# One gate projection of a hybrid decoder layer moved from the opening into the last three query pairs of the attention

## The chip, the cores and the metric

The kernel runs on one core of a Trainium2 chip. A core has a matrix engine (PE, TensorE), a vector engine (DVE), a scalar engine (ACT, ScalarE), a general engine (POOL, GpSimd) and an engine that here only issues transfers (SP, SyncE). Each engine takes its instructions in a fixed order and waits at the head of its queue for what an instruction needs. The metric is the device time of one execution in microseconds (us); lower is better.

## The reference, cut to what matters

One layer runs on a prompt of 1,024 tokens and on 8 sequences of 4 new tokens (1,056 tokens in all). A combined input projection feeds an attention and a gated recurrence; a shared output projection and a feed-forward part follow. The change touches `lg`, the gate of the recurrence:

```
u = rmsnorm(x, p['g_norm1']) * (1 + sc1) + sh1
proj = u @ p['w_in']
q, k, v, lx, lg = jnp.split(proj, [...], axis=-1)
...
hs, h_last = rg_lru(xc, h0, p['w_rgate'], ..., p['lru_lambda'])
lru_out = (hs * jax.nn.gelu(lg.astype(F32), approximate=True)).astype(dt)
m = jnp.concatenate([attn_out, lru_out], axis=-1) @ p['w_out']
```

`lg` has 512 channels, so four tiles of 128 channels; each is a projection of its own, and only `lru_out`, the second half of the input of the output projection, needs it. The recurrence `hs` itself does not.

## The kernel before, in words

Every float32 operand of a projection is kept as a high and a low half, and every product is made of three matmuls (lines 156 to 158). `Weights` takes the weight matrices ("units") one after another in a fixed list: it loads a unit raw, splits it on ScalarE (`w_hi`, line 60) and GpSimd (`w_lo`), and puts the halves into one of four slots, chosen by the unit's place in the list. A projection of one gate tile covers 128 channels and all 1,056 tokens, in three token chunks of 384, 384 and 288 (`TC`): 8 products of 3 matmuls for each chunk, 72 matmuls in all.

The program runs in this order, and a scheduler that weighs times beforehand fixes each engine's order:

1. The opening: normalisation, input projections of the recurrence (`lx`), gate projections (`pj`), the two value blocks (`v_ps`), the first query and key groups (`qk_ps`). The recurrence runs behind it tile by tile: gate matmuls `pg`, chains of elementwise work, a scan (line 541). `proj(4)`, `proj(7)` and `proj(10)` project gate tiles 0, 1 and 2 there, `gelu(n, b)` takes the gelu on ScalarE (line 551), and `lru_out(n)` multiplies it by the scanned `T2[n]` on DVE (lines 557 to 561) and stores the product in `scr_l[n]`. Tile 3's scan is stored alone, in `scr_h` (line 590).
2. The attention over 16 query pairs g = 0 to 15 (4 heads of 4 pairs; a later pair of a head sees more keys). `score` makes the scores `s_ps` (lines 804 to 806), ScalarE takes the exponential `p_e` (line 813), DVE combines the two halves, PE transposes them (`qk_pt`, line 834), and `pv` multiplies them by the values (`pv_ps`). Two banks hold scores, so the next scores wait until an exponential has read its bank. Up to pair 12 the gaps of a pair are filled with matmuls of the queries and keys of pair g + 3 (`qk_mm`). The last pairs have no such fill. Gate tile 3 fills there instead: `lg_piece` projects half of the inner dimension of one token chunk into a bank named `qk_ps`, and after the second half takes the gelu (tile `gl`, line 869) and stores it in `scr_l[3]`. Chunk 0 is put into pair 14 and chunks 1 and 2 into pair 15.
3. The output projection (`wo_k`, `wo_ps`). `lru_cat_stage` brings the recurrence's half of its input back for a token chunk: for each tile m it loads `cat` from `scr_l[m]`, for m = 3 also `hs` from `scr_h`, multiplies the two on DVE (line 998) and splits the product into `act_h` (ScalarE, line 1000) and `act_l` (line 1001). Chunk 0 is staged during the last pairs, chunks 1 and 2 later, with a two-buffer pool that `cat` and `hs` share. The key pages of the 32 new tokens (`kp`, line 1004) are loaded in the same stretch on SP's queue, into buffers that hold parts of the projection's input until the last gate piece has read them.
4. The feed-forward part, over half of the span.

Exponential and gelu use different tables of ScalarE: each change between them is an `ACT_TABLE_LOAD` in the trace.

Of the kernel before, what the change touches and what calls it, by code (L numbers as in the profile page):

```python
# [6 lines left out]
F32 = mybir.dt.float32  # L7
# [9 lines left out]
SEQ = 1024  # L17
NS = 8
DT = 4
# [20 lines left out]
class Weights:  # L40
# [12 lines left out]
    def split_to(self, n, eng=None):  # L53
        while len(self.parts) < min(n, len(self.units)):
            i = len(self.parts)
            self.dma_to(i + 1)
            s = i % 4 if i < 12 else 2 if i == 12 else (3, 2, 0, 1)[(i - 13) % 4]
            hi = self.pool.tile([128, 1024], F32R, name="w_hi", tag=f"w_hi{s}", bufs=1)
            lo = self.pool.tile([128, 1024], F32R, name="w_lo", tag=f"w_lo{s}", bufs=1)
            self.nc.scalar.activation(hi, self.raw[i], AF.Copy)  # L60
            (eng or self.nc.gpsimd).tensor_tensor(lo, self.raw[i], hi.bitcast(F32), op=ALU.subtract)  # L61
            self.parts.append((hi, lo))
            self.dma_to(i + 1 + RAW)
# [82 lines left out]
class Build:  # L146
# [25 lines left out]

    def run(self):
        a = self.a
        units = [a["w_in"][i] for i in (0, 1, 2, 3, 4, 7, 8, 5, 11, 12, 6, 9, 10, *range(13, 20))] + [a["w_out"][i] for i in (4, 5, 6, 7, 0, 1, 2, 3)]
        order = [("u", 0), ("u", 1), ("u", 2), ("u", 3)]
        for b in range(NFF // 2):
            if b + 1 < NFF // 2:
                order += [("u", 4 * b + 4), ("u", 4 * b + 5)]
            order += [("d", 2 * b), ("d", 2 * b + 1)]  # L180
            if b + 1 < NFF // 2:
                order += [("u", 4 * b + 6), ("u", 4 * b + 7)]
        self.ffn_unit = {o: len(units) + i for i, o in enumerate(order)}
        units += [a["w_up"][i] if t == "u" else a["w_down"][i] for t, i in order]
        with self.pool("const") as cp, self.pool("weights") as wp, self.pool("acts") as ap_:
            self.cp, self.ap, self.act = cp, ap_, {}
            self.W = Weights(self.nc, wp, units)
            self.front()
            self.output()
# [13 lines left out]
    def front(self):  # L203
# [362 lines left out]
        def lru():  # L566
            yield from conv(0)
            yield from conv_split(0)
            yield from conv(1)
            yield from gates(0)  # L570
            yield from conv_split(1)
            yield from chain(0)
            while 2 not in X:
                yield None
            yield from conv(2)
            yield from gates(1)
            yield from conv_split(2)
            yield from chain(1)
            yield from gates(2)
            yield from lru_out(0)  # L580
            while 3 not in X:
                yield None
            yield from conv(3)
            yield from conv_split(3)
            yield from lru_out(1)
            yield from chain(2)
            yield from gates(3)
            yield from lru_out(2)
            yield from chain(3)
            SP.dma_start(a["scr_h"], T2[3])  # L590

        W.split_to(4)
        evac(0, lx01[0])
# [50 lines left out]
            return b.rearrange("p (x c) -> p x c", x=2)  # L644

        def v_block(bl, hook):
            unit = (5, 11)[bl]
            vh, vl = (v01[bl][:, z] for z in range(2))
            for pr in range(4):
                p = two(bank("v_ps", "mm", MM[0]))  # L650
                for x in range(2):
                    for hf in range(2):
                        project_half(p, x, 2 * pr + x, unit, hf)
                st = stage("v_st")
                S.activation(st, p, AF.Copy)
                S.dma_start(a["v_o"][pr][:, :, bl * 256:(bl + 1) * 256], st)
                S.activation(vh[:, 2 * pr:2 * pr + 2], p, AF.Copy)
                V.tensor_tensor(vl[:, 2 * pr:2 * pr + 2], p, vh[:, 2 * pr:2 * pr + 2].bitcast(F32),
                                op=ALU.subtract)
                hook(pr)  # L660
            p = two(bank("v_ps", "mm", MM[0]))
            for hf in range(2):
                project_half(p, 0, 8, unit, hf)
            S.activation(self.vsn[:, bl * 256:(bl + 1) * 256], p[:SAMP, 0], AF.Copy)

        v_block(0, lambda pr: None)
        W.split_to(11)
        b = proj(7)
        gelu(1, b)
        W.split_to(12)  # L670
        gqk = self.load(vp, "g_qk", [128, 2, 64])
        cs = self.load(vp, "rope", [128, 9, 2, 16])
        g64 = "p x (g d) -> p (x g) d"
# [36 lines left out]
        tbank = [lambda: bank("qk_pt", "mm", MM[0])]  # L710

        def qk_unit(h):
            return 11 + 2 * h if h else 8

        def qk_mm(g, piece):

# [34 lines left out]
        for g in range(3):  # L751
            for i in range(4):
                qk_mm(g, i)
            qk_norm(g)
            if g == 1:
                b = proj(10)
                bg.until(lambda: 3 in T2 and len(done) >= 6)
                gelu(2, b)
                W.split_to(13)
        bg.finish()  # L760
        lpp.__exit__(None, None, None)
        SP.dma_start(a["lru_h_o"], lho)
# [15 lines left out]
        SP.dma_start(mk, a["maskT"])  # L778
        G.tensor_copy(idb, ident)
        G.tensor_copy(mkb, mk)  # L780
        W.split_to(15)
        qk_T(0)
        psp.__exit__(None, None, None)

# [71 lines left out]
                S.activation(ot, PO.pop(g), AF.Copy)  # L856
                S.dma_start(a["scr_o"][h][:, pr * 256:(pr + 1) * 256], ot)

        def lg_piece(i, half):
            t0, tw = TC[i]  # L860
            hi, lo = W.get(19, NK)
            if half == 0:
                PS["lg"] = qbank[0]()
            b = PS["lg"]
# [2 lines left out]
            if half:  # L867
                t = stage("gl3").rearrange("p x c -> p (x c)")
                S.activation(t[:, :tw], b[:, :tw], AF.Gelu_apprx_tanh)
                S.dma_start(a["scr_l"][3][:, t0:t0 + tw], t[:, :tw])  # L870

        NG = 4 * H
        for _ in range(2):
# [3 lines left out]
        for g in range(NG):  # L877
            h, pr = divmod(g, 4)
            if g + 3 < NG:
                fill = [lambda i=i: qk_mm(g + 3, i) for i in range(4)]  # L880
            else:
                fill = [lambda i=i, j=j: lg_piece(j, i) for j in ((),(0,),(1,2))[g + 3 - NG] for i in range(2)]
            nT = (g - 1) % 4 + 1 if g else 0
            Ts = [lambda b=b: pv_T(g - 1, b) for b in range(nT)]
            Ps = [lambda b=b: pv(g - 1, b) for b in range(nT)]
# [5 lines left out]
            if pr == 2:  # L891
                b = qbank[0]()
                for hf in range(2):
                    project_half(two(b[:, :512]), 0, 8, qk_unit(h), hf)
                W.split_to((17, 19, 21, 23)[h])
                ss = stage("qk_ss")
                ys = sums(b[:SAMP, None, :256], 1, SAMP, ss[:SAMP, 0:1])
            if h < 2:
# [6 lines left out]
            if g == 9:  # L905
                self.x2 = [x2p.tile([128, 4, T], F32, name="x2a", tag="v", bufs=1)]
                SP.dma_start(self.x2[0], a["xT"][0:4].rearrange("m p t -> p m t"))
            if g == NG - 1:
                early = [self.lru_cat_load(0, stage, m) for m in range(2)]
            score(g, 0, 0)  # L910
            score(g, 0, 1)
# [72 lines left out]
    def lru_cat_stage(self, i, stage, early=()):  # L984
# [3 lines left out]
        s = slice(t0, t0 + tw)  # L988
        for m in range(4):
            t = early[m] if m < len(early) else self.lru_cat_load(i, stage, m)  # L990
            if m == 3:
                hs = stage("hs3").rearrange("p x c -> p (x c)")[:, :tw]
                SP.dma_start(hs[:, :w], a["scr_h"][:, t0:t0 + w])
                if tw > w:
                    sv = bass.AP(tensor=a["scr_h"].tensor, offset=a["scr_h"].offset + SEQ + 3,
                                 ap=[[LO, 128], [7, NS], [1, DT]])
                    SP.dma_start(hs[:, w:].rearrange("p (s q) -> p s q", s=NS), sv)
                V.tensor_tensor(t, t, hs, op=ALU.mult)
            hi, lo = self.act_at(4 + m, s)
# [663 lines left out]
```

## Time and profile before

| what | before |
|---|---|
| runs of the kernel | 1361.44, 1362.48 and 1366.3 us, median 1362.48 |
| the profiled execution: its own time | 1362.76 us |
| the profiled execution: its span in the trace | 1360.2 us |
| granted clock of PE, mean | 0.995 |
| PE, DVE, ACT, POOL busy | 1312.9, 777.0, 552.1, 480.0 us |
| last exponential of pair 15 ends | 439.10 us |
| output projection's second group begins | 453.86 us |

The span runs from the first to the last instruction that the profiler recorded; the profiled execution's own time is 2.56 us longer. Times within the trace, such as 439.10, are counted from the span's start. Busy shares are means over stages that differ a lot, so the rows below are read stage by stage.

### The profile page before, as it was taken

The page shows a single profiled execution, that of the slowest core. Times are in us where ns is not written, and L with a number is a line of the kernel's source. Part 1 is how long each engine was busy: PE and PEld are TensorE (multiplying, and loading weights), DVE is VectorE, ACT ScalarE, POOL GpSimd, SP SyncE. Part 2 cuts the span into 40 slices and gives each one's busy share as a digit, 9 for nine tenths or more (in the row PEclk, how much of TensorE's full clock was granted, in tenths as well). Part 3 has the DMA queues.
Part 4 walks back from the last instruction along what each step waited for, and adds up shares of the span by engine and source line. Part 5 has one row for each costly group of instructions (what it writes and reads, how often), then busy time and mean ns, then how long its engine had stood idle before and what let it go on. Part 6 is the DMA issues. An engine that isn't in the chain of part 4 may idle for free.

```text
span 1360.2 us, 23560 instructions
## 1 busy us (share of the span) xinstructions
PE 1312.9 (97%) x9488; PEld 1271.0 (93%) x9488; DVE 777.0 (57%) x1399; ACT 552.1 (41%) x975; POOL 480.0 (35%) x581
## 2 busy tenths in 40 slices
PE   4999999999998999999999999999999999999998
PEld 3889999989998877999999999999999999999998
DVE  5767543767676455967645354545454554545366
ACT  4355554666677222457233332323232323232311
POOL 0442144857673024327232323223232323232310
PEclk9999999999998999999999999999999999999999
DMA  9865213101315656021111211111111111121103
GB/s 367 299 232 198 68 43 116 48 25 44 119 47 171 243 186 225 1 76 58 37 63 32 61 33 49 46 47 47 47 47 47 47 45 49 32 62 32 54 9 140
DMA packets 50686, 122.16 MB, mean 90 GB/s; under 512 B 7282, under 2 KB 24306, under 8 KB 47506
## 3 DMA queue, kind: packets, MB, share of 16 engines
q1 hardware_dynamic: 45666, 115.93, 25.5%
q10 hardware_dynamic: 4912, 4.74, 1.0%
q8 instruction: 74, 1.21, 0.4%
q14 instruction: 34, 0.28, 0.1%
HBM read 106.70 MB, written 13.94 MB: 89 GB/s over the span
## 4 chain that ended last, share of the span: by engine, by line
PE 89%; ACT 4%; DVE 3%; DMA 2%; issue 1%; POOL 0%; SPq 0%; ACTq 0%; DVEq 0%
PE up L156 13%; PE up L157 12%; PE up L158 12%; PE dn L156 6%; PE dn L158 6%; PE dn L157 6%; PE qk_ps L156 2%; PE wo_ps L156 2%; PE wo_ps L158 2%; PE qk_ps L157 2%; PE qk_ps L158 2%; PE wo_ps L157 2%; PE v_ps L157 1%; PE v_ps L158 1%; PE v_ps L156 1%; PE pj L156 1%
## 5 line engine op out<-in xcount | busy, mean ns | idle before, releaser
L61 POOL TENSOR_TENSOR w_lo<-w_raw,w_hi 128x1024 fp32r<-128x1024 f32 x88 | 216.6, 2468 | 547.9 <-ACT w_hi L60 498.9
L156 PE MATMUL up<-act_h,w_hi 128*128 128x384 f32 (+1 forms) x1056 | 341.4, 325 | 2.0 <-ACT act_h L1192 2.0
L158 PE MATMUL up<-act_h,w_lo 128*128 128x384 f32 (+1 forms) x1056 | 340.1, 322 | 1.6 <-DVE w_lo L61 1.6
L157 PE MATMUL up<-act_l,w_hi 128*128 128x384 f32 (+1 forms) x1056 | 340.7, 323 | 0.0
L1394 DVE SCALAR_TENSOR_TENSOR fy<-fx,conv_ffn_w,fy 128x1072 f32<-128x1072 f32 (+2 forms) x92 | 137.4, 1494 | 165.0 <-ACT fy L1392 163.7
L60 ACT ACTIVATE w_hi<-w_raw 128x1024 fp32r<-128x1024 f32 x94 | 98.4, 1058 | 264.1 <-PE dn L157 151.7
L156 PEld LDWEIGHTS up<-act_h,w_hi 128*128 128x128 f32 x1056 | 197.9, 188 | 2.4 <-ACT act_h L1192 2.3
L158 PEld LDWEIGHTS up<-act_h,w_lo 128*128 128x128 f32 x1056 | 198.3, 188 | 1.9 <-DVE w_lo L61 1.9
L157 PEld LDWEIGHTS up<-act_l,w_hi 128*128 128x128 f32 x1056 | 198.3, 188 | 0.3 <-DVE act_l L1198 0.3
L156 PE MATMUL dn<-hh,w_hi 128*128 128x384 f32 (+1 forms) x528 | 171.0, 324 | 0.0
L158 PE MATMUL dn<-hh,w_lo 128*128 128x384 f32 (+1 forms) x528 | 170.4, 323 | 0.0
L157 PE MATMUL dn<-hl,w_hi 128*128 128x384 f32 (+1 forms) x528 | 170.0, 322 | 0.0
L1152 DVE SCALAR_TENSOR_TENSOR x2a<-dn,modT,x2a 128x384 f32<-128x384 f32 (+1 forms) x132 | 74.7, 568 | 98.8 <-PE dn L158 98.8
L1152 DVE SCALAR_TENSOR_TENSOR x2b<-dn,modT,x2b 128x384 f32<-128x384 f32 (+1 forms) x132 | 75.4, 573 | 69.7 <-PE dn L158 69.5
L156 PEld LDWEIGHTS dn<-hh,w_hi 128*128 128x128 f32 x528 | 99.2, 188 | 0.0
L157 PEld LDWEIGHTS dn<-hl,w_hi 128*128 128x128 f32 x528 | 99.2, 188 | 0.0
L158 PEld LDWEIGHTS dn<-hh,w_lo 128*128 128x128 f32 x528 | 99.1, 188 | 0.0
L156 PE MATMUL qk_ps<-w_hi,act_h 128*128 128x256 f32 (+1 forms) x288 | 83.1, 289 | 1.2 <-ACT qk_sq L681 1.2
L157 PE MATMUL qk_ps<-w_lo,act_h 128*128 128x256 f32 (+1 forms) x288 | 82.5, 286 | 0.0
L158 PE MATMUL qk_ps<-w_hi,act_l 128*128 128x256 f32 (+1 forms) x288 | 81.5, 283 | 0.0
L157 PE MATMUL wo_ps<-act_l,w_hi 128*128 128x384 f32 (+1 forms) x192 | 62.9, 328 | 0.0
L156 PE MATMUL wo_ps<-act_h,w_hi 128*128 128x384 f32 (+1 forms) x192 | 62.6, 335 | 0.0
(337 smaller groups left out, 2656.2 us busy)
## 6 DMA issues: line engine op xcount, KB each, us to landing
w_ada<-w_ada SPq DMA_DIRECT2D x24, 1024.0 KB, 6.8
w_raw<-w_up SPq DMA_DIRECT2D x44, 512.0 KB, 3.6
w_raw<-w_down SPq DMA_DIRECT2D x22, 512.0 KB, 3.6
w_raw<-w_in SPq DMA_DIRECT2D x20, 512.0 KB, 4.1
page<-cache_v SPq DMA_DIRECT2D x32, 256.0 KB, 5.6
xT<-xT SPq DMA_DIRECT2D x8, 528.0 KB, 7.8
w_raw<-w_out SPq DMA_DIRECT2D x8, 512.0 KB, 3.7
kp<-cache_k SPq DMA_DIRECT2D x16, 256.0 KB, 4.8
```

Source lines behind the costliest of these rows:

```text
L60: self.nc.scalar.activation(hi, self.raw[i], AF.Copy)
L61: (eng or self.nc.gpsimd).tensor_tensor(lo, self.raw[i], hi.bitcast(F32), op=ALU.subtract)
L156: self.PE.matmul(out, lh, rh, start=first, stop=False)
L157: self.PE.matmul(out, lh, rl, start=False, stop=False)
L158: self.PE.matmul(out, ll, rh, start=False, stop=last)
L1152: V.scalar_tensor_tensor(x2(m, t0, t0 + w), b[:, :w], gt[:, m, 0:1], x2(m, t0, t0 + w), op0=ALU.mult, op1=ALU.add)
L1394: post.append(lambda c0=c0, c1=c1, j=j: V.scalar_tensor_tensor(y[:, c0:c1], x[:, c0 + j:c1 + j], fw[:, ci, j:j + 1], y[:, c0:c1], op0=ALU. ...
```

## The change

Gate tile 2 is no longer projected in the opening: `proj(10)`, `gelu(2, b)` and `lru_out(2)` go, and its scan is stored in `scr_h[0]` as tile 3's is in `scr_h[1]`. Tiles 2 and 3 are both projected by `lg_piece`, two pieces in each of pairs 13, 14 and 15, in the order (tile 2, chunk 0), (tile 3, chunk 0), (2, 1), (2, 2), (3, 1), (3, 2). `lru_cat_stage` multiplies both tiles by a loaded `hs`. The list of units and the rule of the slots follow, and `W.split_to(23)` moves to the head of pair 15.

```diff
-            s = i % 4 if i < 12 else 2 if i == 12 else (3, 2, 0, 1)[(i - 13) % 4]
+            s = (i if i < 12 else i + 2) % 4
...
-            yield from lru_out(2)
+            SP.dma_start(a["scr_h"][0], T2[2])
             yield from chain(3)
-            SP.dma_start(a["scr_h"], T2[3])
+            SP.dma_start(a["scr_h"][1], T2[3])
...
             if g == 1:
-                b = proj(10)
-                bg.until(lambda: 3 in T2 and len(done) >= 6)
-                gelu(2, b)
-                W.split_to(13)
+                W.split_to(12)
...
-        def lg_piece(i, half):
+        def lg_piece(n, half):
+            m, i = ((0, 0), (1, 0), (0, 1), (0, 2), (1, 1), (1, 2))[n]
             t0, tw = TC[i]
-            hi, lo = W.get(19, NK)
+            hi, lo = W.get(18 + m, NK)
...
-                SP.dma_start(a["scr_l"][3][:, t0:t0 + tw], t[:, :tw])
+                S.dma_start(a["scr_l"][2 + m][:, t0:t0 + tw], t[:, :tw])
...
-                fill = [lambda i=i, j=j: lg_piece(j, i) for j in ((),(0,),(1,2))[g + 3 - NG] for i in range(2)]
+                fill = [lambda i=i, j=j: lg_piece(j, i) for j in ((0, 1), (2, 3), (4, 5))[g + 3 - NG] for i in range(2)]
...
-                W.split_to((17, 19, 21, 23)[h])
+                W.split_to((16, 18, 20, 22)[h])
...
             if g == NG - 1:
+                W.split_to(23)
                 early = [self.lru_cat_load(0, stage, m) for m in range(2)]
...
-            if m == 3:
+            if m > 1:
+                sh = a["scr_h"][m - 2]
                 hs = stage("hs3").rearrange("p x c -> p (x c)")[:, :tw]
-                SP.dma_start(hs[:, :w], a["scr_h"][:, t0:t0 + w])
+                SP.dma_start(hs[:, :w], sh[:, t0:t0 + w])
```

Three places of the engines' orders are shown; lines of the changed kernel are 1 to 4 lower than those of before.

On PE, in the opening, this is the last part of gate tile 2's projection (`pj`) with the gate matmuls of tile 3 (`pg`) inside it, before the change:

```order
L158 MATMUL pj_1945<-act_h_64,w_lo 128x288
L156 MATMUL pj_1945<-act_h_64,w_hi 128x288
L156 MATMUL pg<-xh,wgh 128x360
L157 MATMUL pg<-xl,wgh 128x360
L158 MATMUL pg<-xh,wgl 128x360
...
L158 MATMUL pg<-xh,wgl 128x360
L157 MATMUL pj_1945<-act_l_65,w_hi 128x288
```

With the change the same `pg` matmuls stand between those of a query and key group and of the second value block:

```order
L156 MATMUL qk_ps<-w_hi,act_h_64 128x256
L157 MATMUL qk_ps<-w_lo,act_h_64 128x256
L156 MATMUL pg<-xh,wgh 128x360
L157 MATMUL pg<-xl,wgh 128x360
L158 MATMUL pg<-xh,wgl 128x360
L158 MATMUL qk_ps<-w_hi,act_l_65 128x256
...
L158 MATMUL v_ps<-w_hi,act_l_65 128x256
L156 MATMUL pg<-xh,wgh 128x360
```

No `pj` row of gate tile 2 is left there, and the `pg` rows have moved among rows that were behind it.

On ACT, around the exponentials of pairs 14 and 15 before the change (tiles carry the buffer's number; 768 and 896 columns are keys):

```order
L813 ACTIVATE p_e_5313,le_1391<-s_ps_5303,ls_5311 128x768
L869 ACT_TABLE_LOAD
L869 ACTIVATE gl3_5480<-qk_ps_5432 128x384
L870 DMA scr_l<-gl3_5480 128x384
L813 ACT_TABLE_LOAD
L813 ACTIVATE p_e_5374,ls_5311<-s_ps_5365,ls_5311 128x768
L813 ACTIVATE p_e_5417,le_1391<-s_ps_5405,ls_5415 128x896
L60 ACTIVATE w_hi_5610<-w_raw_5244 128x1024
L869 ACT_TABLE_LOAD
```

With the change, from the exponential of 384 columns in pair 13 on and again at the head of pair 15:

```order
L809 ACTIVATE p_e_5062,ls_5051<-s_ps_5055,ls_5051 128x384
L866 ACT_TABLE_LOAD
L866 ACTIVATE gl3_5127<-qk_ps_5064 128x384
L867 DMA scr_l<-gl3_5127 128x384
L809 ACT_TABLE_LOAD
L809 ACTIVATE p_e_5093,le_1391<-s_ps_5085,ls_5091 128x512
...
L809 ACTIVATE p_e_5342,ls_5279<-s_ps_5333,ls_5279 128x768
L866 ACT_TABLE_LOAD
L866 ACTIVATE gl3_5315<-qk_ps_5249 128x384
```

From the first exponential of pair 13 to the last of pair 15 three gelus with three pairs of table loads stood before, and four gelus with four pairs stand now; the other two gelus, of the last two pieces, follow the last exponential, behind one more load.

On SP, from the first key pages on, before the change (`cat` and `hs` are those of token chunk 0):

```order
L1004 DMA kp<-cache_k 128x512
...
L981 DMA cat<-scr_l 128x384 x2
L1004 DMA kp<-cache_k 128x512
...
L993 DMA hs_5585<-scr_h 128x384
L1004 DMA kp<-cache_k 128x512
```

and with the change:

```order
L1002 DMA kp<-cache_k 128x512
...
L979 DMA cat<-scr_l 128x384
L992 DMA hs_5583<-scr_h 128x384
L979 DMA cat<-scr_l 128x384
L1002 DMA kp<-cache_k 128x512
...
L992 DMA hs_5590<-scr_h 128x384
L1002 DMA kp<-cache_k 128x512
```

Four key pages stand ahead of the `cat` of tile 2 in both. On PE the last gate piece stood ahead of the last rounds of scores before; now it stands behind all scores and behind the first 8 matmuls of the output projection.

## Rows read from the trace of the kernel before

**Rows 1.** The page, part 1: busy time, share of the span, instructions.

```profile
PE 1312.9 (97%) x9488; PEld 1271.0 (93%) x9488; DVE 777.0 (57%) x1399; ACT 552.1 (41%) x975; POOL 480.0 (35%) x581
```

**Rows 2.** Waits of PE over the span: total us, times, longest.

```profile
PE s_ps L804 <- DVE QA L746: 4.6, 4, 2.1
PE s_ps L804 <- ACT p_e L813: 4.4, 5, 2.7
```

**Rows 3.** Windows: length; busy PE, PEld, DVE, ACT, POOL; clock; DMA share; GB/s.

```profile
158.37:169.99 11.62, 11.62 (x75) 11.62 (x74) 0.00 (x0) 3.59 (x5) 4.75 (x2) 1.00 0.30 92
...
201.70:227.25 25.55, 25.55 (x219) 25.41 (x218) 9.32 (x13) 6.50 (x11) 8.12 (x15) 1.00 0.32 111
700.00:1360.00 660.00, 656.43 (x4074) 656.20 (x4072) 333.50 (x558) 192.89 (x279) 185.87 (x200) 1.00 0.16 49
```

**Rows 4.** Timeline: tile 3's scan, the attention's first transpositions; start, duration.

```profile
205.32 2.41 DVE L541 TENSOR_TENSOR_SCAN t<-xc,t 128x1080 f32<-128x1080 f32 x1
...
227.25 0.49 PE L733 MATMUL qk_pt<-ident,qk_st 128*128 128x128 f32 x3
```

**Rows 5.** Windows of the last pairs, columns as in rows 3.

```profile
394.77:453.86 59.09, 52.58 (x354) 50.38 (x354) 37.79 (x70) 37.36 (x73) 22.48 (x34) 0.91 0.44 146
398.92:439.10 40.18, 33.93 (x221) 32.16 (x220) 26.69 (x45) 31.78 (x64) 18.99 (x30) 0.88 0.46 147
439.10:453.86 14.76, 14.50 (x100) 14.21 (x98) 7.89 (x17) 3.47 (x8) 0.54 (x3) 0.98 0.52 183
422.79:440.50 17.71, 15.03 (x82) 14.36 (x83) 11.02 (x19) 12.95 (x22) 5.70 (x11) 0.71 0.73 240
```

**Rows 6.** Timeline of PE, pairs 14 and 15; idle before in brackets.

```profile
416.26 0.34 PE L157 MATMUL qk_ps<-act_l,w_hi 128*128 128x384 f32 x1
416.44 0.33 PE L158 MATMUL qk_ps<-act_h,w_lo 128*128 128x384 f32 x1
...
420.10 0.38 PE L156 MATMUL pv_ps<-pTh,v 128*128 128x256 f32 x1 [1.71 <-DVE QA L746]
```

**Rows 7.** Windows of 2 us, columns as in rows 3.

```profile
418.00:420.00 2.00, 0.39 (x4) 0.20 (x2) 1.41 (x3) 1.94 (x6) 1.58 (x4) 1.00 0.00 0
...
434.00:436.00 2.00, 2.00 (x10) 1.91 (x11) 1.93 (x4) 2.00 (x5) 0.00 (x0) 0.50 0.95 354
```

**Rows 8.** ACT by line, 398.9 to 439.1: busy us, mean ns, idle before.

```profile
L869 ACT ACT_TABLE_LOAD x3 | 3.8, 1283 | 0.1
L813 ACT ACT_TABLE_LOAD x3 | 3.8, 1283 | 1.5 <-ACT oT L856 0.6 <-ACT act_h L1000 0.5 <-ACT gl L869 0.4
...
L1000 ACT ACTIVATE act_h<-cat 128x384 fp32r<-128x384 f32 x4 | 2.1, 527 | 1.6 <-DMA cat<-scr_l 1.6
...
L869 ACT ACTIVATE gl<-qk_ps 128x384 f32<-128x384 f32 (+1 forms) x3 | 1.4, 466 | 0.0
```

**Rows 9.** Timeline of ACT: the end of the last exponential of pair 15.

```profile
438.89 0.21 ACT L813 ACTIVATION_READ_ACCUMULATOR p_e<-s_ps,ls 128x1 f32 x1
```

**Rows 10.** Timeline of SP: the first four key pages.

```profile
426.06 1.94 SPq L1004 DMA_DIRECT2D kp<-cache_k  x4
```

**Rows 11.** DMA issues, 425 to 445: KB each, median us to landing.

```profile
kp<-cache_k SPq DMA_DIRECT2D x16, 256.0 KB, 4.8
```

**Rows 12.** Timeline: tile 3 of token chunks 1 and 2, and its first readers.

```profile
475.01 0.32 SPq L993 DMA_DIRECT2D hs<-scr_h  x1
...
479.99 0.56 DVE L998 TENSOR_TENSOR cat<-cat,hs 128x384 f32<-128x384 f32 x1 [3.01 <-DMA hs<-scr_h]
...
481.18 1.02 POOL L1001 TENSOR_TENSOR act_l<-cat,act_h 128x384 fp32r<-128x384 f32 x1 [7.56 <-ACT act_h L1000]
...
484.70 0.34 PE L156 MATMUL wo_ps<-act_h,w_hi 128*128 128x384 f32 x1
...
504.28 0.81 POOL L1001 TENSOR_TENSOR act_l<-cat,act_h 128x288 fp32r<-128x288 f32 x1 [1.46 <-ACT act_h L1000]
...
509.12 0.29 PE L157 MATMUL wo_ps<-act_l,w_hi 128*128 128x288 f32 x1
```

More of the change, by code (lines that the diff above doesn't have):

```diff
@@ L174, in run @@
         a = self.a
-        units = [a["w_in"][i] for i in (0, 1, 2, 3, 4, 7, 8, 5, 11, 12, 6, 9, 10, *range(13, 20))] + [a["w_out"][i] for i in (4, 5, 6, 7, 0, 1, 2, 3)]
+        units = [a["w_in"][i] for i in (0, 1, 2, 3, 4, 7, 8, 5, 11, 12, 9, 10, *range(13, 19), 6, 19)] + [a["w_out"][i] for i in (4, 5, 6, 7, 0, 1, 2, 3)]
         order = [("u", 0), ("u", 1), ("u", 2), ("u", 3)]
@@ L646, in v_block @@
         def v_block(bl, hook):
-            unit = (5, 11)[bl]
+            unit = (5, 10)[bl]
             vh, vl = (v01[bl][:, z] for z in range(2))
@@ L666, in front @@
         v_block(0, lambda pr: None)
-        W.split_to(11)
+        W.split_to(10)
         b = proj(7)
         gelu(1, b)
-        W.split_to(12)
         gqk = self.load(vp, "g_qk", [128, 2, 64])
@@ L712, in qk_unit @@
         def qk_unit(h):
-            return 11 + 2 * h if h else 8
+            return 10 + 2 * h if h else 8
         def qk_mm(g, piece):
@@ L780, in front @@
         G.tensor_copy(mkb, mk)
-        W.split_to(15)
+        W.split_to(14)
         qk_T(0)
@@ L869, in lg_piece @@
                 S.activation(t[:, :tw], b[:, :tw], AF.Gelu_apprx_tanh)
-                S.dma_start(a["scr_l"][3][:, t0:t0 + tw], t[:, :tw])
+                S.dma_start(a["scr_l"][2 + m][:, t0:t0 + tw], t[:, :tw])
         NG = 4 * H
@@ L990, in lru_cat_stage @@
             t = early[m] if m < len(early) else self.lru_cat_load(i, stage, m)
-            if m == 3:
+            if m > 1:
+                sh = a["scr_h"][m - 2]
                 hs = stage("hs3").rearrange("p x c -> p (x c)")[:, :tw]
-                SP.dma_start(hs[:, :w], a["scr_h"][:, t0:t0 + w])
+                SP.dma_start(hs[:, :w], sh[:, t0:t0 + w])
                 if tw > w:
-                    sv = bass.AP(tensor=a["scr_h"].tensor, offset=a["scr_h"].offset + SEQ + 3,
-                                 ap=[[LO, 128], [7, NS], [1, DT]])
+                    sv = bass.AP(tensor=sh.tensor, offset=sh.offset + SEQ + 3, ap=[[LO, 128], [7, NS], [1, DT]])
                     SP.dma_start(hs[:, w:].rearrange("p (s q) -> p s q", s=NS), sv)
@@ L1641 @@
         args[k] = nc.dram_tensor(k, (4, 128, n), F32, kind="Internal").ap()
-    args["scr_h"] = nc.dram_tensor("scr_h", (128, LO), F32, kind="Internal").ap()
+    args["scr_h"] = nc.dram_tensor("scr_h", (2, 128, LO), F32, kind="Internal").ap()
     with tile.TileContext(nc, schedule_with_timeline_sim=True) as tc:
```

## The prediction, made before the changed kernel had run

> **What bounds the kernel now.** I read the busy times first: PE is busy for 97% of the span, no other engine for more than 57% [rows 1]. So the time is PE's work plus PE's gaps, and a change that adds and removes equal work can win only in the gaps. Windows then show where there are any. The feed-forward stage has 656.43 us of PE work in 660.00, and the two stretches of the opening that matter here have no idle time at all: 11.62 of 11.62 and 25.55 of 25.55 [rows 3]. In the last three pairs it is different: from 394.77 to 453.86 PE works 52.58 of 59.09 us at a mean granted clock of 0.91 [rows 5]. That is 6.51 us of idle time, and a second loss inside the busy time: from 422.79 to 440.50 the granted clock is 0.71, so the stretch holds what full speed would do in 0.71 × 17.71 = 12.57 us, less the idle time; 5.1 us go to the clock. The list of waits says who is late: the scores wait 4.6 us for the copies of the queries on DVE and 4.4 us for the exponential of ScalarE [rows 2], and in pair 14 one such gap before `pv` is 1.71 us [rows 6]. A pair with no filler matmuls stalls: in 418 to 420 PE works 0.39 of 2 us, and after the gaps of pair 15 the next 2 us run at 0.50, the lower of its levels (1.2 of 2.4 GHz) [rows 7]. So this stage has at most 6.5 + 5.1 = 11.6 us to give.
>
> **The opening loses one projection.** A gate projection is 72 matmuls. The window of gate tile 1's is 11.62 us long and full [rows 3]; tile 2's has the same shapes, and I take 11.62 for it too (0.161 a matmul; a 384-column one takes 416.44 − 416.26 = 0.18, a 288-column one three quarters of that). The 18 `pg` matmuls that were mixed into it stay. It gave cover to tile 3's chain of gate matmuls, exponentials and scan, so the question is whether PE then waits. The scan ran from 205.32 to 207.73, and PE's next other stage, the attention's first transposition, came at 227.25 [rows 4]. With 11.62 us less it comes at 215.6; the scan, even if it moved not at all, has ended 7.9 us before that, and its store has still that time to land before the pools are reused. The chain will rather move forward, since DVE loses 2 us of multiplication and ScalarE three gelus and their table loads. I take **−11.62**, with nothing for a stall; a late scan could cost no more than the few us by which it passed 215.6, for which no row gives a reason.
>
> **The last pairs get the work back.** How much of the 11.62 us shows there depends on three things. First ScalarE, from the first exponential of pair 13 to the last of pair 15, 40.18 us [rows 5]. It works 31.78 of them and stands on the chain that paces the scores: scores, maximum on DVE, exponential, scores again, with two banks. Its own load is 3 gelus of 0.47, 6 table loads of 1.28, and 1.5 us of waiting ahead of the loads that bring the exponential back (0.1 ahead of the others) [rows 8]. By the orders four gelus lie between those exponentials now: one more gelu and two more loads, 0.47 + 2 × 1.28 + a third of 1.5 = 3.5 us of ScalarE, and one conversion `act_h` (0.53) goes behind the last exponential: 3.0 more. From below it is 0: ScalarE has 8.4 us free there, and the fills put matmuls into gaps of PE that keep the clock up. From above it is 3.4, all of it on the chain. On PE four pieces stand there in place of three: 24 more matmuls of 0.175, 4.2 us, into 40.18 − 33.93 = 6.25 idle us, so PE isn't the limit. I take the middle, **+1.5**, because two of the loads fall in pair 13, whose exponentials are the shortest, and because ScalarE is busy for only 79% of the stretch.
>
> **What stands behind the last exponential.** Before, that was 14.76 us to the second group of the output projection, 14.50 of them PE work [rows 5, 9]. Now PE does there: the last piece, 24 × 0.134 = 3.2; 40 matmuls of the first group, 40 × 0.175 = 7.0; about 30 `pv` matmuls of 256 columns, 30 × 0.117 = 3.4; 15 transpositions, 15 × 0.11 = 1.65 (three took 0.49 with the drain of the last [rows 4]). The last piece cannot start at once: its bank is read by the gelu of the piece before it, which stands behind the last exponential and a table load, 1.28 + 0.47 = 1.75 [rows 8]. Ahead of the piece PE has only 12 `pv` matmuls, 5 transpositions and 8 matmuls of the output projection, and the wait for the last exponential uses these up, so the 1.75 counts. The piece's first matmuls release the buffers of the key pages. Four pages are issued in 1.94 us [rows 10] and land 4.8 later [rows 11]; the `cat` and `hs` of tile 2 are queued behind them on SP. From that release S the product of tile 2 is ready at S + 2.0 + 5.4 (`cat` and `hs` land together, a bit later than a page) + 0.57 + 0.53 + 0.56 + 0.3 for handing over = S + 9.4. PE has other work until S + 7.2 by the order (the second half of the piece, 16 matmuls of the output projection, 12 transpositions and 13 of `pv`: 1.6 + 2.8 + 1.3 + 1.5). So a stall of about 2.1 us arises at the third block of the first group, on a load that was hidden before. 1.75 + 3.2 + 7.0 + 3.4 + 1.65 + 2.1 = 19.1, **+4.3** on 14.76. From below 0: the loads land sooner or the release comes while the scores still run. From above +7: pages land late and the stall reaches 5.
>
> **The output projection's later chunks.** One more load and product for each of chunks 1 and 2, with two shared buffers. Before, tile 3's product of chunk 1 was split by 482.20 and read at 484.70, 2.5 us of slack; of chunk 2 by 505.09 and read at 509.12, 4.0 of slack [rows 12]. The new `hs` takes the place in the queue where tile 3's `cat` stood, so the trips overlap in part. I take **+0.5**; above, a whole trip for each is 7.2 us (issue 475.01 to split 482.20), which is rival D.
>
> **The sum.** −11.62 + 1.5 + 4.3 + 0.5 = −5.3. The profiled execution took 1362.76 us (its span 1360.2 and 2.56 around it), 0.3 over the median of the runs, 1362.48. That gives 1357.5.
>
> **The table loads, by the rows and by a rule.** The rows charge a switch 1.28 for the load and, for the way back only, 0.4 to 0.6 of waiting ahead of it; the loads of the gelu's table waited 0.1 in all [rows 8]. The Trainium skill, "ScalarE: Activation LUTs", section "What ACT_TABLE_LOAD costs", gives about 1.28 us for the load and about 1.38 for a drain ahead of it, some 2.66 for a switch. The load agrees with the trace, the drain does not show. By that rule two more switches and a gelu would be 5.8 us instead of 3.5 and, all on the chain, would turn the +1.5 into some +5.3, an end near 1361; that is rival C, and the measured waits speak against it.
>
> **The rivals.** *B, the gaps absorb all.* The six pieces fill the gaps, PE doesn't fall to the lower level, and the work returns at no price: the 6.5 idle us and the 5.1 of the clock are just 11.6. Then −11.62 + 0.5, about 1351.6. For it: the dips at 418 and at 432 to 436 are where a piece was missing [rows 7]. Against: the last piece stands behind the scores, where before there were 0.26 us idle of 14.76. *C, nothing gained.* ScalarE's extra 3.4 all shows, and the wait behind the exponentials is 7: −11.62 + 3.4 + 7 + 0.5 = −0.7, 1362.0. For it: 4.4 us of the scores' waits are ScalarE's already [rows 2]. Against: 8.4 us free. A clock fall during the new wait for `hs` (as after the gap at 432 to 434 [rows 7]) would add some 3 to 4 and end in the same place. *D, slower.* The two shared buffers make the loads of tile 2 and tile 3 follow each other in chunks 1 and 2: each trip of 7.2 us comes on top, less the slacks of 2.5 and 4.0 [rows 12]: 4.7 + 3.2 = 7.9, in place of +0.5: −5.3 − 0.5 + 7.9 = +2.1, 1364.9. It decides once the second trip starts later than the first's end by more than the slack. Against it: `hs` is issued as soon as a buffer falls free, where `cat` of tile 3 was. *The change doesn't do what it says:* if tile 3's chain held PE in the opening for as long as the projection took, the opening would gain nothing; that ends above 1366, and the full windows of PE leave it 2 in 100.
>
> **How the numbers follow.** My forecast has 0.50, with its own range of 1354 to 1361 (the bounds of the terms, not all on one side); B 0.25; C 0.15; D 0.08; the last 0.02. The range of 8 in 10 reaches from just below B to D's lower edge, 1351.0 to 1364.5. A difference of 0.5% is 6.8 us, about what a measurement tells from none: faster by more than that means below 1355.7, which takes all of B and about a quarter of my own case: 0.37. Slower by more than 6.8 needs D with the bounds of other terms at their upper ends, or the last case: 0.05. The rest, 0.58, lies within 0.5%.
>
> **What would show it.** Right: PE full from the first query and key matmul of the second group to the first transposition, which comes near 215.6; the first exponential of pair 13 to the last of pair 15 in 40 to 44 us with no 0.50 in the windows before the last exponential; from there to the second group 17 to 21 us, with one wait of PE on the product of tile 2 (`act_h` or `act_l`) of about 2 us; no wait of PE above 1 us in chunks 1 and 2. Wrong: a wait on `t` or `e` in the opening; s_ps waits on the exponential well over 4.4 us (C); a wait on the products in chunk 1 or 2 of several us (D); a stretch at the lower level behind the scores; or no wait at all behind the last exponential (B).

## The result, and the profile after

The changed kernel is slower: 1371.29 us median of 7 runs (1368.82 to 1372.34) against 1363.13 for 7 runs of the kernel before (1361.44 to 1366.3). The ratio is 1.0051, with a 95% interval of 1.0041 to 1.0062. The forecast was 1357.5, with a range up to 1364.5, so it missed by 14 us (1371.29 against 1357.5) and on the wrong side. The profiled execution took 1372.34 us, its span is 1370.0: 9.8 more than the span before.

The page, part 1, of the changed kernel:

```profile
PE 1321.9 (96%) x9488; PEld 1270.6 (93%) x9488; DVE 778.7 (57%) x1399; ACT 554.2 (40%) x977; POOL 482.1 (35%) x581
```

Against [rows 1] PE has the same 9488 matmuls and is busy for 9.0 us more. Nothing was added to PE's work, so some matmuls must have become dearer; that is the first thing to see, and it says that the loss of 9.8 us over the span isn't idle time in the main.

Next, where the lead is won and lost. The timeline of the changed kernel shows the first transposition of the attention (227.25 before [rows 4]) and the last exponential of pair 15 (439.10 before [rows 9]):

```profile
215.57 0.60 PE L732 MATMUL qk_pt<-ident,qk_st 128*128 128x128 f32 x4
...
427.95 0.20 ACT L809 ACTIVATION_READ_ACCUMULATOR p_e<-s_ps,ls 128x1 f32 x1
```

The lead, by how much the changed kernel is ahead, is 11.68 us at the start of the attention and still 10.95 at the end of the last exponential. Windows of the changed kernel follow, with the columns of [rows 3]: first exponential of pair 13 to the last of pair 15; from there to the second group of the output projection; and from that group to the first matmul of the feed-forward part. The second fence is the last of these stretches in the kernel before.

```profile
389.36:428.07 38.71, 36.73 (x266) 35.14 (x264) 25.28 (x44) 34.72 (x64) 15.43 (x20) 1.00 0.28 85
428.07:448.31 20.24, 18.14 (x129) 17.85 (x128) 7.93 (x17) 7.76 (x16) 5.08 (x11) 1.00 0.75 234
...
448.31:594.18 145.87, 141.09 (x1072) 109.63 (x1071) 85.34 (x261) 41.96 (x94) 40.87 (x36) 0.98 0.47 156
```

```profile
453.86:583.53 129.67, 129.22 (x1073) 107.42 (x1072) 81.71 (x253) 40.78 (x94) 40.10 (x36) 1.00 0.47 158
```

The pairs went from 40.18 to 38.71 us although they hold more (266 matmuls in place of 221), and the granted clock rose from 0.88 to 1.00 [rows 5]. The stretch behind them grew from 14.76 to 20.24. At the second group the lead was still 5.55 us (453.86 against 448.31). Then the rest of the output projection took 145.87 us in place of 129.67: **16.2 us lost in a stretch in which the change adds one load and one product for each of two token chunks**.

What is longer there: I summed, for each kind of matmul in that stretch, the time from its start to the next matmul's start, so with any wait behind it (before, after, in us): `wo_ps` 90.1 and 94.9, `sa_po` 14.5 and 20.3, `o_bc` 3.2 and 7.0, `o_ms` 8.6 and 10.2. These four are 16.0 of the 16.2. `sa_po` is the product of the new tokens' probabilities with the values, for four sequences at a time. Four matmuls take the new tokens' own values (`vsn`); then, for each of four places, four matmuls take the pages of cached values, one page to a sequence, each with 16 output partitions. These 16 are called value-page matmuls here. The trace shows each matmul as two records. The rows for it, by line from 440 to 560, before and then after:

```profile
L1105 PE MATMUL sa_po<-page,sa_pts 128*16 128x512 f32 x64 | 13.0, 596 | 0.3 <-DMA page<-cache_v 0.3
```

```profile
L1103 PE MATMUL sa_po<-page,sa_pts 128*16 128x512 f32 x64 | 20.7, 596 | 0.0
```

One record lasts 596 ns in both, the count is 64 in both, and no wait is added; only the busy time, which counts overlapping records once, rose from 13.0 to 20.7. So before, more of the matmuls overlapped than after. The timelines of PE show it, before first:

```profile
475.15 1.05 PE L1101 MATMUL sa_po<-vsn,sa_pts 32*16 32x512 f32 x8
476.13 1.91 PE L1105 MATMUL sa_po<-page,sa_pts 128*16 128x512 f32 x16
477.97 0.44 PE L156 MATMUL wo_ps<-act_h,w_hi 128*128 128x384 f32 x1
```

```profile
467.96 1.05 PE L1099 MATMUL sa_po<-vsn,sa_pts 32*16 32x512 f32 x8
468.94 1.40 PE L1103 MATMUL sa_po<-page,sa_pts 128*16 128x512 f32 x5
...
474.30 1.03 PE L1103 MATMUL sa_po<-page,sa_pts 128*16 128x512 f32 x2
475.26 0.44 PE L157 MATMUL wo_ps<-act_l,w_hi 128*128 128x384 f32 x1
475.54 0.34 PE L158 MATMUL wo_ps<-act_h,w_lo 128*128 128x384 f32 x1
475.72 0.34 PE L156 MATMUL wo_ps<-act_h,w_hi 128*128 128x384 f32 x1
475.98 1.03 PE L1103 MATMUL sa_po<-page,sa_pts 128*16 128x512 f32 x2
476.94 0.45 PE L157 MATMUL wo_ps<-act_l,w_hi 128*128 128x384 f32 x1
```

Before, eight matmuls (16 records) took 476.13 to 477.97, 0.92 for four. After, one alone between matmuls of the output projection (128 output partitions) takes 474.30 to 475.26: 0.96. Four in a row cost what one costs alone. Of the first 16 value-page matmuls, in PE's order, 8 and 3 stand together before and five alone; in the changed kernel 3 and 2 stand together and eleven alone.

The waits of PE in the changed kernel, over the span, add two things:

```profile
PE s_ps L800 <- DVE QA L745: 4.6, 4, 2.1
PE wo_ps L156 <- ACT act_h L998: 4.1, 2, 2.1
...
PE s_ps L800 <- ACT p_e L809: 1.9, 3, 0.9
```

The scores' wait for the exponential fell from 4.4 to 1.9 [rows 2], and the output projection now waits twice for `act_h`, about 2.1 each. One of the two is the stall that the forecast expected in the first group. The other, at 495.64, is the product of tile 3 in chunk 1. Its `hs` had landed at 485.83, and the product came only at 494.02. The timeline of DVE says why:

```profile
490.79 0.61 DVE L1293 SCALAR_TENSOR_TENSOR cat<-cat,gsubT,o_bc 128x384 f32<-128x384 f32 x1 [7.07 <-PE o_bc L1291]
491.76 0.71 DVE L1113 SCALAR_TENSOR_TENSOR sa_o<-sa_po,hmask,sa_o 16x128 f32<-16x128 f32 x2 [0.35 <-PE sa_po L1103]
...
494.02 1.02 DVE L996 TENSOR_TENSOR cat<-cat,hs 128x384 f32<-128x384 f32 x1
```

DVE sat idle for 7.07 us in front of an instruction that waits for PE's `o_bc`, and the product stood behind it in DVE's queue. PE in turn came to that `o_bc` only at 490.20; three single value-page matmuls, 0.96 each, stood ahead of it among others. PE then waited 2.04 us for the product, and the clock fell; this is the window of the next 12 matmuls of the output projection:

```profile
495.64:499.78 4.14, 4.13 (x12) 3.70 (x13) 3.49 (x10) 1.80 (x4) 2.78 (x3) 0.50 0.48 146
```

They took 4.14 us at the lower of the two levels (granted clock 0.50), where 12 take 2.1 at full speed (12 × 0.175).

### The profile page after: what moved, and what is told of

Read it like the earlier page. It is cut to its first block, busy times and chain, and to the rows that moved or that the text cites. A ratio compares the mean times of both kernels' runs of the same rounds, so it can differ in the third digit from the quotient of the medians.

```text
span 1370.0 us, 23554 instructions
## 1 busy us (share of the span) xinstructions
PE 1321.9 (96%) x9488; PEld 1270.6 (93%) x9488; DVE 778.7 (57%) x1399; ACT 554.2 (40%) x977; POOL 482.1 (35%) x581
## 4 chain that ended last, share of the span: by engine, by line
PE 88%; ACT 4%; DVE 3%; DMA 3%; issue 1%; SPq 0%; POOL 0%; ACTq 0%; DVEq 0%
PE up L156 13%; PE up L157 12%; PE up L158 12%; PE dn L156 6%; PE dn L158 6%; PE dn L157 6%; PE qk_ps L156 3%; PE qk_ps L157 3%; PE qk_ps L158 3%; PE wo_ps L156 2%; PE wo_ps L157 2%; PE wo_ps L158 2%; PE sa_po L1103 1%; PE v_ps L157 1%; PE s_ps L800 1%; PE v_ps L158 1%
```

## The experiments

Ratios are to runs of the kernel before, timed beside each variant, with 95% intervals; 1% is 13.6 us. The changed kernel stands at 1.0051.

**First: loads or release?** My first two theories were both about transfers: theory L, the second `hs` load and product through two shared buffers; theory P, the late release of the key pages' buffers.

`one_hs`: tile 2's `hs` and product left out in token chunks 1 and 2.

```diff
-            if m > 1:
+            if m > 1 and (m == 3 or i == 0):
```

> This kernel is the changed one, but in token chunks 1 and 2 the load of hs for tile 2 and its product are left out (tile 2 goes on without its scan there; chunk 0 is as changed). Theory L (the loss of some 15 us behind the first group of the output projection comes from the second hs load and product in chunks 1 and 2, through the two shared buffers): 1357 to 1360 us, the first product of chunk 1 gone and the third block of its second group no longer waited for. Theory P (the last gate piece, behind the scores, holds the buffers of the key pages, so that all page loads slide against PE, and the order of the value-page matmuls breaks up): 1367 to 1371, little changed.

Measured: 1366.26 us, 1.0010 (0.9994 to 1.0025). That is 5.6 us less than the changed kernel (0.41% of 1364), and neither what L said nor what P said.

`cst3`: a third buffer for `cat` and `hs`.

```diff
-            return p.tile([128, 2, 192], F32, name=name, tag="cst", bufs=2)
+            return p.tile([128, 2, 192], F32, name=name, tag="cst", bufs=3)
```

> The changed kernel with three buffers instead of two for cat and hs in the output projection, nothing left out. Theory L: the trips of tile 2 and tile 3 overlap again, 1358 to 1362. Theory P: 1367 to 1371, as the changed kernel.

Measured: 1366.46 us, 1.0017 (1.0001 to 1.0032), 4.6 us less. So the shared buffers are a cost, and the third buffer is worth as much as leaving the load out. In its trace the stretch from the second group on is 10.5 us shorter than the changed kernel's 145.87:

```profile
453.53:588.86 135.33, 133.95 (x1072) 107.71 (x1071) 81.94 (x261) 41.36 (x94) 40.09 (x36) 1.00 0.49 163
```

The time doesn't gain as much, because this execution, the slowest of its ten, came to the second group at 453.53, 5.2 us later. The sums in it are 17.6 for `sa_po`, and 3.5 for `o_bc`, about as before the change. So what the buffers cost isn't cleanly apart from the order of the matmuls.

`early321`: the pieces 3, 2, 1 over pairs 13, 14, 15.

```diff
-                fill = [lambda i=i, j=j: lg_piece(j, i) for j in ((0, 1), (2, 3), (4, 5))[g + 3 - NG] for i in range(2)]
+                fill = [lambda i=i, j=j: lg_piece(j, i) for j in ((0, 1, 2), (3, 4), (5,))[g + 3 - NG] for i in range(2)]
...
+            if g == NG - 3:
+                for _ in range(2):
+                    pop(fill)
```

> The changed kernel with the six gate pieces spread 3, 2, 1 over pairs 13, 14 and 15 in place of 2, 2, 2; everything else as changed. Theory P: the key pages start some 8 us earlier against the end of the scores, the stall at the third block of the first group goes, the value-page matmuls stand in fours again, and the time falls to 1353 to 1359. Theory L: the loads of chunks 1 and 2 are as before, so only the stall of 2 us and some of the work behind the scores goes: 1366 to 1369.

Measured: 1363.74 us, 0.9998 (0.9984 to 1.0011). The time lies between the two, and for another reason than either gives. Its windows, the output projection from the second group on, and below it the pairs (first exponential of 13 to the last of 15):

```profile
453.14:584.54 131.40, 131.03 (x1072) 107.81 (x1072) 81.99 (x261) 40.37 (x94) 40.19 (x36) 1.00 0.48 161
396.49:442.37 45.88, 40.81 (x294) 38.44 (x292) 24.30 (x42) 39.58 (x70) 17.56 (x25) 1.00 0.39 123
```

The pairs took 45.88 us in place of 38.71, with ScalarE busy for 39.58, and ate the lead; PE came to the second group at 453.14, as late as before, and behind it the loss was nearly gone: 131.40 against 129.67, with the value-page matmuls about as cheap as before (busy for 13.7 us; 13.0 before). This turned the question from transfers to the order that the scheduler makes of these matmuls.

`by_tile`: tile 2's three pieces ahead of tile 3's.

```diff
-            m, i = ((0, 0), (1, 0), (0, 1), (0, 2), (1, 1), (1, 2))[n]
+            m, i = ((0, 0), (0, 1), (0, 2), (1, 0), (1, 1), (1, 2))[n]
```

> The changed kernel with the six pieces in the order tile 2 chunks 0, 1, 2, then tile 3 chunks 0, 1, 2, so that the first chunk of tile 3 comes fourth and not second. Both theories: no change beyond 2 us, 1369 to 1373, since the last piece is the same one at the same place; if the first chunks had to be ahead, the wait on the product of tile 3 in chunk 0 grows by the time from one piece to the fourth, and the time goes over 1375.

Measured: 1373.36 us, 1.0067 (1.0049 to 1.0084): as the changed kernel. That both first chunks stand ahead of the others is worth nothing that shows.

**Second: keeping the four together by force.** In four kernels the four matmuls of a place were put in a critical section, a block that the scheduler doesn't break up.

```diff
+                with self.tc.tile_critical():
                     for j in range(4):
                         PE.matmul(po[32 * j:32 * j + 16], pts[:, pg, 16 * j:16 * j + 16], vt[j], start=False, stop=(pg == 3))
```

> The changed kernel with the four matmuls of a value page kept together on PE, so that nothing stands between them; nothing left out. In the traces so far four such matmuls in a row take 0.94 us together and one between others 0.96 alone. Theory F (what is lost behind the first group is lost to this order: the singles): their sum falls from 20.3 us to some 10 and the time by 6 to 10, to 1361 to 1366. Theory P (the page loads set the pace): the time saved turns into waits for pages, 1368 to 1372.

> The kernel before with the same four matmuls kept together. Theory F: their sum falls from 14.5 us to some 10, the time by 3 to 5, to 1358 to 1361. Theory P: within 2 us of before.

> The changed kernel with the gate pieces spread 3, 2, 1 and the four matmuls of a value page kept together. Theory F: 4 to 5 us under the 3, 2, 1 kernel, so 1358 to 1361, level with the kernel before in fours. Theory P: 1362 to 1366.

> The changed kernel with three buffers for cat and hs and the four matmuls of a value page kept together. If both the shared buffers and the singles cost and nothing else does, 6 to 8 us under the three-buffer kernel, 1357 to 1361, under before. Theory P: 1364 to 1369.

Measured: 1.0149 (1.0113 to 1.0184), 1.0118 (1.0087 to 1.0148), 1.0132 (1.0100 to 1.0163) and 1.0158 (1.0126 to 1.0190). All are slower by 16 to 22 us than the kernel before. The waits of PE in `before_four` say that the section itself is the reason: between 440 and 610, PE waits 15.6 us in all at its matmuls, where the kernel before waits 0.3. Two of the rows:

```profile
PE sa_po L1106 <- DMA page<-cache_v: 6.5, 2, 3.2
...
PE sa_po L1106 <- DMA w_raw<-w_up: 4.5, 2, 2.9
```

The section waits there not only for its pages but also for transfers that its matmuls don't read, such as the feed-forward part's weights. These runs decide nothing between the theories.

**Third: the same, with one added wait.** Here only the first of the four waits for the last page of its place; nothing else is held.

```diff
-                    PE.matmul(po[32 * j:32 * j + 16], pts[:, pg, 16 * j:16 * j + 16], vt[j], start=False, stop=(pg == 3))
+                    mm = PE.matmul(po[32 * j:32 * j + 16], pts[:, pg, 16 * j:16 * j + 16], vt[j], start=False, stop=(pg == 3))
+                    if j == 0:
+                        self.tc.add_manual_dep(mm.ins, landed["v", g, pg].ins.name, mybir.DependencyInfo(
+                            mybir.DependencyClass.Sync, mybir.DependencyReason.DATA), reason="whole page")
```

> The changed kernel in which the first matmul of a value page's four waits for all four pages of its place, so that the scheduler puts the four in a row; nothing else is held and nothing is left out. Theory F (behind the first group much of the loss is the value-page matmuls taken singly, 0.96 us each against 0.94 for four in a row): their sum falls from 20.3 to about 10 us, the time by 6 to 10, to 1361 to 1366. Theory P (page loads set the pace): waits of PE on pages appear in place of it, 1368 to 1372.

> The kernel before with the same wait for all four pages of a place. Theory F: the sum of these matmuls falls from 14.5 to about 10, the time by 3 to 5, to 1358 to 1361. Theory P: within 2 us of before.

> The changed kernel with three buffers for cat and hs and the wait for all four pages of a place. If shared buffers and singles are the two causes, both are gone and the gain of the opening shows against the kernel before with the same wait: 1354 to 1358. If a third cause is left, 1360 to 1366.

> The changed kernel with the pieces spread 3, 2, 1 and the wait for all four pages of a place. Singles are fewer here (14.7 us in all), so by theory F 4 us under the 3, 2, 1 kernel, about 1360, level with before in the same form; by theory P no change, 1363 to 1365.

Measured: `after_whole` 1360.38 us, 0.9967 (0.9951 to 0.9984); `before_whole` 1360.09 us, 0.9975 (0.9958 to 0.9993); `cst3_whole` 1356.06 us, 0.9949 (0.9931 to 0.9967); `early_whole` 1359.05 us, 0.9959 (0.9942 to 0.9977). By this one wait the changed kernel gets faster by 0.84 points of a per cent (1.0051 to 0.9967), 11.5 us, the kernel before by 3.4. So 8.1 us of it answer to the change; with the wait in both, the two kernels take the same time (1360.38 and 1360.09). The rows by line, 440 to 560, of `after_whole`, then `before_whole`:

```profile
L1105 PE MATMUL sa_po<-page,sa_pts 128*16 128x512 f32 x64 | 8.2, 596 | 2.2 <-DMA page<-cache_v 2.2
```

```profile
L1107 PE MATMUL sa_po<-page,sa_pts 128*16 128x512 f32 x64 | 7.8, 596 | 0.5 <-DMA page<-cache_v 0.5
```

The busy time falls from 20.7 and 13.0 to 8.2 and 7.8, and 2.2 us of waits for pages come in its place in the changed kernel. Theory F named the right cause; its size, 6 to 10 us, came out for the kernel before (3 to 5 expected, 3.4 measured) and was too small for the changed one (11.5). Of theory P 2.2 us are left. In `after_whole` the timeline has all four of a place in one row:

```profile
475.29 1.05 PE L1105 MATMUL sa_po<-page,sa_pts 128*16 128x512 f32 x8
```

The stretch from the second group to the feed-forward part, of `after_whole`, `before_whole` and `cst3_whole`:

```profile
450.05:580.79 130.74, 125.29 (x1072) 106.85 (x1071) 82.34 (x261) 41.44 (x94) 40.59 (x36) 1.00 0.50 172
```

```profile
451.98:578.99 127.01, 125.30 (x1073) 106.66 (x1072) 83.86 (x255) 40.63 (x94) 41.37 (x36) 1.00 0.48 162
```

```profile
447.95:576.90 128.95, 124.93 (x1072) 107.06 (x1071) 85.15 (x261) 41.37 (x94) 41.04 (x36) 1.00 0.51 174
```

145.87 has become 130.74, 15.1 us less. By the sums of starts 10.7 of them are `sa_po` (20.3 to 9.7) and 4.7 are `wo_ps` (94.9 to 90.2), where the fall of the clock behind the product at 495 is gone. (The wait changes the scheduler's order in other places as well, so only the 10.7 are traced to these matmuls themselves.) `o_bc` and `o_ms`, 5.4 us of the 16.2, did not go: they stand at 7.1 and 10.4. The kernel before loses 2.7 us in this stretch by the same wait (129.67 to 127.01), so with the wait in both, the changed kernel's is longer by 3.7 us in place of 16.2. PE is now busy for the same 125.3 us in both; what is left is idle time.

**Fourth: what the move is worth without these costs.** Before with both cures, and the changed kernel with both and its last two pieces one step earlier in pair 15:

```diff
+            if g == NG - 1:
+                for _ in range(2):
+                    pop(fill)
```

> The kernel before with both cures, the wait for all four pages and three buffers for cat and hs. It has one hs load for a token chunk, so by the theory that two loads through two buffers cost, the third buffer is worth nothing here: 1359 to 1362, level with the kernel before with the wait alone. If it falls to 1356 as the changed kernel did with both cures, the gate's move itself is worth nothing.

> The changed kernel with both cures, and the last two gate pieces one step earlier in pair 15, so that the last one stands ahead of the last scores and the key pages' buffers fall free sooner. By the forecast's fourth step (the stall on the product of tile 2 behind a late release) it gains up to 2 us on the same kernel without it: 1354 to 1357. If the scores then wait for the pieces instead, as in the 3, 2, 1 spread, 1358 to 1362.

Measured: `before_both` 1360.77 us, 0.9981 (0.9968 to 0.9995), and `head_both` 1357.05 us, 0.9949 (0.9933 to 0.9965). In the kernel before the third buffer is worth nothing (0.9975 without it). The moved gate with both cures is 0.9949 against 0.9981, 4.4 us faster, and the intervals (0.9931 to 0.9967, 0.9968 to 0.9995) just don't meet; `cst3_whole` and `before_both` were not timed beside each other, so this rests on the two ratios. `head_both` and `before_both` were: 1357.05 and 1360.77 us, ratios of 0.9949 (up to 0.9965) and 0.9981 (from 0.9968). Placing the last piece earlier changed nothing in the time. All six kernels with the added wait are a little faster than both kernels, with intervals that end below 1; `cst3_whole` and `head_both` are the fastest.

## Why the prediction was wrong, point by point

- **The opening, −11.62.** Right: −11.68 at the first transposition. No wait took the projection's place.
- **The last pairs, +1.5.** Wrong in sign, and near in the sum by luck. From the first exponential of pair 13 to the last of pair 15 the time fell by 1.47 us (40.18 to 38.71). ScalarE's added load was there (31.78 to 34.72 us busy) and hid; PE's idle time fell from 6.25 to 1.98 us and the half clock of pair 15 (0.71 between 422.79 and 440.50 [rows 5]) did not return, and that paid for the extra matmuls; of rival B this half was right. But the lead was only 9.56 us at the first of these exponentials (398.92 against 389.36): 2.1 us went in the pairs ahead of it, where the forecast had no term. It placed five of the six pieces, four among the exponentials and one behind them. In the trace 101 of the 144 gate matmuls lie among them, 24 behind, and 19 ahead of the first, from 384.28 on; the lead falls by 0.9 there. Another 1.2 went in one stretch between two exponentials of earlier pairs, before and after:

```profile
300.40:305.76 5.36, 4.81 (x41) 4.52 (x42) 4.88 (x10) 4.31 (x12) 2.22 (x3) 1.00 0.08 26
```

```profile
288.75:295.33 6.58, 6.03 (x39) 5.76 (x40) 4.88 (x10) 4.30 (x12) 3.31 (x5) 0.74 0.07 24
```

  The clock fell there in the changed kernel's trace. In the trace of `before_whole`, which has no move, it falls there too (granted 0.50 from 300.5 to 303.9), and in that of `one_hs`, which has the move, it does not; so these runs don't show it as a cost of the move.
- **Behind the last exponential, +4.3.** It measured 20.24 − 14.76 = +5.5, within its bounds. (30 × 0.117 is 3.5 and not 3.4, which changes nothing.) The wait that was forecast came where it was forecast and as long, 2.10 against 2.1; this is the row:

```profile
441.67 0.44 PE L156 MATMUL wo_ps<-act_h,w_hi 128*128 128x384 f32 x1 [2.10 <-ACT act_h L998]
```

- **The output projection's later chunks, +0.5, bounded above by a trip for each chunk. This is the step that failed: +16.2.** I priced a load and a product, looked for their cost on the loads' path, and took the matmuls of this stretch to cost what they cost before. What the runs showed in its place are two costs.
  - *The order of the value-page matmuls.* They stand one by one among those of the output projection, where each costs as much as four. That is 5.8 us of the loss in their own sum, and more behind them: the product of tile 3 came late, PE waited 2.04 us for it, and the clock fell. By the one added wait, which keeps them in fours, 8.1 us of the time (11.5 less the 3.4 of the kernel before) and 12.5 of the stretch's 16.2 are gone. That this order is a cause is shown.
  - *The two shared buffers.* The third buffer takes another 4.3 us off the changed kernel with the wait (1360.38 to 1356.06), and nothing off the kernel before. Together that is 12.4 us, about the distance from the forecast's −5.3 to the +7.0 of the measured ratio; each of the two is good to some 3 us. Which matmuls this cost sits at stays open: `o_bc` is 7.0 in the changed kernel, 7.1 with the wait, 5.1 with the buffer too, 3.5 with the buffer alone.

  Why the order broke up is argued. PE came to the new tokens' part 7 us earlier (467.96 against 475.15), and the value pages did not: the first to be timed in the trace landed at 469.0 (468.7 before), the last of the first sixteen at 480.6 (483.1 before). In the six kernels without the wait, the sum of `sa_po` goes roughly with PE's arrival there: 14.5 us at 475.15, 14.7 at 474.08 (`early321`), 17.6 at 471.91 (`cst3`), 19.2 at 468.11 (`by_tile`), 20.3 at 467.96 and 19.6 at 466.38 (`one_hs`). But the order is fixed beforehand, and the scheduler's own reckoning isn't in the trace.
- **What the terms add up to.** −11.7, +0.7 in all the pairs, +5.5 and +16.2 make the changed kernel 10.7 us late at the feed-forward part (594.18 against 583.53); 0.9 come back behind it, which gives the 9.8 of the span.
- **Rival D** named the right stretch and one of its causes. It had 8 in 100. The two shared buffers cost 4.6 us (`cst3`), where it had 7.9, and even with the load left out altogether (`one_hs`) 5.6 came back: the larger part of the time lost is not a load's.
- **Table loads.** By the rows a switch cost the load and some tenths; by the rule of the Trainium skill ("ScalarE: Activation LUTs", section "What ACT_TABLE_LOAD costs") the forecast had 5.8 us for the added switches and gelu. The changed kernel's loads from the first exponential of pair 13 to the last of pair 15:

```profile
L866 ACT ACT_TABLE_LOAD x4 | 5.1, 1283 | 0.4 <-ACT oT L852 0.4
L809 ACT ACT_TABLE_LOAD x4 | 5.1, 1283 | 0.8 <-ACT gl L866 0.8
```

  Eight loads had 1.2 us of waiting ahead of them in all, and ScalarE was busy for 2.9 us more, so the trace bears out the rows. The Trainium skill gives the drain without saying on which side of the load it lies; the forecast put it ahead. Behind the loads it doesn't show either: the three gelus before the change waited 0.0 [rows 8].
- **What a kernel without the two costs gives** is about 4 us for the move (4.4 by the ratios, 3.7 by the times of `head_both` and `before_both`), where the forecast said 5.3.

## What to carry to other kernels

When a change lets PE arrive earlier at work that is fed by transfers, ask what PE finds there: the lead is only kept if what it works on next comes earlier too, and the order of the work there may come out dearer than waiting would be. Small matmuls that run side by side belong together; a group that waits for its last operand can be worth more than each starting at once. And compare the busy time of a kind of instruction at equal count and equal duration of one: a rise there is lost overlap, which no list of waits shows. When a cure is tried, give it to the kernel before as well: only the difference answers to the change (8.1 of 11.5 us here). And look at each term of a forecast on its own stretch: here one was wrong in sign, and another loss hid it in the sum.

## What the runs showed of the hardware

Four matmuls with 16 output partitions each, written to partitions 0, 32, 64 and 96 of a bank, took 0.92 to 0.98 us in a row and 0.96 for one alone between matmuls of 128 output partitions. The Trainium skill, "TensorE: Matmul & The Clock Gate", Part 3, section "The mechanism", has such matmuls overlap when they lie in different tiles of the array, and its section "Measured speedup vs the span model" gives 2.38 for three; here four gain a factor of 4.0 (0.96 × 4 / 0.96), and these runs add that the gain is gone when a matmul of 128 output partitions stands between them. A small one doesn't cost that. In the changed kernel two records of `o_ms`, with 12 output partitions, run inside the 0.96 of a single value-page matmul (489.24 to 490.20):

```profile
489.24 0.60 PE L1103 MATMUL sa_po<-page,sa_pts 128*16 128x512 f32 x1
489.25 0.39 PE L1273 MATMUL o_ms<-o_sq,sel 128*12 128x128 f32 x2
489.68 0.59 PE L1103 MATMUL sa_po<-page,sa_pts 128*16 128x512 f32 x1
490.20 0.55 PE L1291 MATMUL o_bc<-o_rs,two_rows 128*128 128x128 f32 x3
```

A second point: the waits show less than a third of what the stretch lost. PE was busy for 141.09 of its 145.87 us, so 4.8 us were idle against 0.5 before; the other 11.9 us are longer busy time.
